# TensorE's order within a head pair: left to the scheduler, or written out in the source

## The chip, the cores and the metric

The kernel runs on one core of one Trainium2 chip. The metric is the device time of one execution, in microseconds (us). A core has TensorE (PE in the profile, for matrix products and transposes), VectorE (DVE), ScalarE (ACT), GpSimd (POOL) and SyncE (SP, which issues most loads). Each works through its own list of instructions and waits at an instruction whose inputs, or whose place to write, are not ready. A product goes from SBUF to one of eight PSUM banks of 128 partitions x 512 fp32; VectorE and ScalarE take it from there.

## What is computed

One decoder layer on 1024 tokens of width 1024, in fp32:

```python
h = rms_norm(x, norm_mix)
xa, ga, q, f, v, g, m_a, m_b = split(h @ w_in)            # 8 x 1024 columns
y_a = rg_lru(conv(xa)) * gelu(ga)                         # gated linear recurrence
f_gate = lb + (1 - lb) * sigmoid(f);  k = (1 - lb) * sigmoid(-f)
o = hgrn2(silu(q), k, log(f_gate), v)                     # 8 heads, state decays by f_gate
y_b = rms_norm_per_head(o) * silu(g)
x = x + (sigmoid(m_a) * y_a + sigmoid(m_b) * y_b) @ w_out
x = x + relu(rms_norm(x) @ w_up)**2 @ w_down
return rms_norm(x, norm_final)
```

In `hgrn2` a query at time t meets a key at an earlier time s through a decay, the product of all gates from s+1 to t, for each of 128 channels.

## The kernel before

The mixer is done in two halves of 512 tokens (`c`), each with four head pairs (`p`), so the main loop (lines 652 to 671) makes eight passes, called pairs here. In each, eight projections of 256 columns are made: `v` and `xa` first, then `q`, `f`, `g`, `mb`, `ga`, `ma`. Every large product is fp32 made of three products of rounded parts (`mm3`, lines 113 to 117, called a triple here): high by high, low by high, high by low. One projection (`project`, line 270) is 48 products of 128x512 into two banks, 24 for each of its two weight tiles. Weight tiles are loaded by SP and split into two parts by ScalarE (a cast, L76) and VectorE (a subtraction, L77); there is room for three split tiles, so a tile is split when the one three places before it in the list `ORDER` (line 29) is used up. These splits have raised priority (400, line 90).

`conv` and `rg_lru` (lines 296 and 326) make the gated recurrence. `rg_lru` has for each of its two heads six products into a bank `pr` and six into a bank `pi`, then ScalarE and VectorE steps on the tiles `rw`, `ri` and `rr`, of which there is one each, so that the second head has to wait for the first. Its instructions have raised priority (300).

`f_of` makes the gate and the key. `hgrn` (line 385) works out the decayed scores at growing block sizes: products for single tokens (`pt1`, L460), for blocks of 2 (`pt2`, L461) and of 8 (`pt8`, L479), 32 small products each; then of 32 (L513, 16 products) and 64 (L525, 8). A product of unrounded fp32 counts as two instructions in the trace. VectorE makes the operands in a chain of multiplications (L388), from one size to the next, and puts the scores together in `dd` with masks (L410, L418). Then, for each head, keys are transposed (`pk`, L551) and copied by ScalarE (`kT`, L553), multiplied with the values to state products (`pkv`, L557), which VectorE adds up to states (`sn`, L571 and L573), and the outputs are made from scores and states (`po`, L564 and L567). ScalarE and VectorE normalise the output (`on`), and it is transposed back (`poT`, L612).

`gates` (line 587) makes the four projections `g`, `mb`, `ga`, `ma` and their nonlinear functions, and joins everything into the mixer's output.

PSUM has four banks under the tag `pj` (projections and `rg_lru`), two under `sc` (scores) and two under `hg` (transposes, states, outputs). A bank is handed on when the last reader of its old contents is through.

What sets the order: the tile framework orders every engine's list when the program is built. An instruction counts as ready by a model of the chip, and among those ready the one earliest in the source (or of raised priority) is taken. So the products of `hgrn` go between the products of `gates` where the model says that their inputs are ready. Only the score blocks are held somewhat: `together` (line 381) puts each block behind one named VectorE instruction, without a wait of its own, so that a block is issued in one piece.

After the eight pairs come the output projection's second half and a feed-forward network in which large products follow each other (from about 915 us on); it is not touched.

## Time and profile before

| | |
|---|---|
| median of 3 runs | 1618.57 us (1615.73 to 1618.93) |
| the profiled execution | 1616.99 us, of it 1615.2 us span from the first to the last instruction |
| PE busy | 1569.3 us in 9240 instructions |
| DVE, ACT, POOL busy | 1214.4, 770.4, 68.0 us |
| one pair | 107.1 us (`q` begins at 148.52 and at 255.63 us) |

A row of the timeline has the start, the duration, engine, line, operation, the tile written and the tiles read, the shape and the number of instructions; in brackets how long the engine was idle before it and what it is thought to have waited for. PE's durations are modelled and overlap: the time that a product takes of the engine is the distance to the next start. A row of the waits has the engine and line that waited, what for, the sum, how many waits, and the longest. A row of the windows has a stretch of the span, its length, then for each engine the busy time and the number of instructions, the granted clock, the share of the DMA engines and GB/s.

### The profile page before, as it was taken

Reading aid. Unit: us, or ns where it says so; the run is one execution under the profiler, and the core shown is the slowest. Engines: PE = TensorE matmul, PEld = TensorE weight load, DVE = VectorE, ACT = ScalarE, POOL = GpSimd, SP = SyncE. Lnnn points to the kernel's source line nnn. Section 1 sums busy time; section 2 is a strip of 40 time slices with the busy share of each in tenths; the row PEclk is TensorE's granted clock in tenths of the full one; section 3 lists DMA queues with packets and bytes.
Section 4 is the critical chain, followed back from the end, with each engine's and each line's share of the span. In section 5 each row is a group of like instructions: output and inputs, shape, how many; then the busy total and the mean of one; then the engine's idle time right before and its main releaser. Section 6 shows DMA issues by size and latency. Waiting matters only on the chain.

```text
span 1615.2 us, 23207 instructions
## 1 busy us (share of the span) xinstructions
PE 1569.3 (97%) x9240; PEld 1306.0 (81%) x9240; DVE 1214.4 (75%) x1751; ACT 770.4 (48%) x1202; POOL 68.0 (4%) x99
## 2 busy tenths in 40 slices
PE   7999999999999999999999997999999999999998
PEld 6878788788788888788788875888888878888886
DVE  5975966848763865947758688888888888788876
ACT  4643545436432544546435476677667732222113
POOL 0010010100100010100100100000000000000000
PEclk9999999999999999999999999999999999999999
DMA  6222223222244222222122362666666575666652
GB/s 238 92 66 92 92 66 103 81 79 91 80 162 138 92 66 92 92 73 97 66 92 92 106 233 78 257 244 242 244 257 242 225 283 214 256 258 249 258 211 105
DMA packets 57996, 246.51 MB, mean 153 GB/s; under 512 B 6688, under 2 KB 6816, under 8 KB 47136
## 3 DMA queue, kind: packets, MB, share of 16 engines
q1 hardware_dynamic: 56304, 239.27, 40.7%
q10 hardware_dynamic: 1584, 5.77, 1.0%
q8 instruction: 72, 1.18, 0.3%
q14 instruction: 36, 0.29, 0.1%
HBM read 185.24 MB, written 59.77 MB: 152 GB/s over the span
## 4 chain that ended last, share of the span: by engine, by line
PE 76%; DVE 20%; DMA 1%; issue 1%; ACT 1%; POOL 0%; DVEq 0%; POOLq 0%; SPq 0%; ACTq 0%
PE dX L115 3%; PE uX L115 3%; PE dX L116 3%; PE dX L117 3%; PE uX L117 3%; PE uX L116 3%; DVE wL L77 3%; PE pv L116 2%; PE pv L117 2%; PE pv L115 2%; PE pj_ma L117 2%; PE pj_ma L115 2%; PE pj_ma L116 2%; PE pj_f L117 2%; PE pj_f L115 2%; PE pj_f L116 2%
## 5 line engine op out<-in xcount | busy, mean ns | idle before, releaser
L77 DVE TENSOR_TENSOR wL<-raw,wH 128x1024 fp32r<-128x1024 f32 x160 | 195.8, 1224 | 136.8 <-ACT wH L76 134.7
L76 ACT CAST wH<-raw 128x1024 fp32r<-128x1024 f32 x160 | 167.8, 1049 | 136.4 <-PE po L116 31.7
L989 DVE TENSOR_TENSOR acc<-acc,dX 128x512 f32<-128x512 f32 x128 | 84.9, 683 | 29.4 <-PE dX L117 29.1
L76 ACT CAST wA<-q 128x512 fp32r<-128x512 f32 x32 | 19.8, 622 | 132.9 <-PE dX L117 101.4
L989 DVE TENSOR_TENSOR acc<-acc,dY 128x512 f32<-128x512 f32 x64 | 43.4, 685 | 15.6 <-PE dY L117 14.6
L345 DVE RECIPROCAL rr<-rr 128x512 f32<-128x512 f32 x16 | 53.5, 3346 | 0.0
L849 ACT ACTIVATE b<-b 128x512 f32<-128x512 f32 x48 | 30.2, 630 | 37.3 <-DVE b L848 37.3
L115 PE MATMUL pv<-wH,hT0H 128*128 128x256 f32 x128 | 37.8, 295 | 0.0
L116 PE MATMUL pv<-wL,hT0H 128*128 128x256 f32 x128 | 37.5, 293 | 0.0
L117 PE MATMUL pv<-wH,hT0L 128*128 128x256 f32 x128 | 37.4, 292 | 0.0
L577 ACT ACTIVATE on<-po 128x128 f32<-128x128 f32 x64 | 17.0, 278 | 41.9 <-PE po L567 41.9
L115 PE MATMUL pv<-wH,hT1H 128*128 128x256 f32 x128 | 36.5, 285 | 0.0
L116 PE MATMUL pv<-wL,hT1H 128*128 128x256 f32 x128 | 36.2, 283 | 0.0
L117 PE MATMUL pv<-wH,hT1L 128*128 128x256 f32 x128 | 36.2, 283 | 0.0
L311 DVE SCALAR_TENSOR_TENSOR xc<-xp,pvt,xc 128x512 f32<-128x512 f32 x48 | 33.1, 745 | 0.0
L596 ACT ACTIVATE smb<-pj_mb 128x512 f32<-128x512 f32 x16 | 9.5, 595 | 46.9 <-PE pj_mb L117 46.9
L850 ACT ACTIVATE b<-b 128x512 f32<-128x512 f32 x48 | 30.0, 630 | 1.1
L491 POOL TENSOR_SCALAR scT<-dd 32x256 f32<-32x256 f32 x32 | 27.6, 863 | 68.3 <-DVE dd L418 66.8
L77 DVE TENSOR_TENSOR wA<-q,wA 128x512 fp32r<-128x512 f32 x32 | 22.0, 687 | 10.4 <-ACT wA L76 9.9
L293 ACT COPY v<-pv 128x256 f32<-128x256 f32 x32 | 11.8, 370 | 30.0 <-PE pv L117 30.0
L116 PE MATMUL pj_ga<-hT0L,wH 128*128 128x512 f32 x64 | 26.1, 408 | 0.0
L117 PE MATMUL pj_ga<-hT0H,wL 128*128 128x512 f32 x64 | 26.1, 408 | 0.0
(1859 smaller groups left out, 5252.2 us busy)
## 6 DMA issues: line engine op xcount, KB each, us to landing
raw<-wts_in SPq DMA_DIRECT2D x160, 512.0 KB, 3.4
q<-mlp_in SPq DMA_DIRECT2D x64, 512.0 KB, 4.0
x<-x_in SPq DMA_DIRECT2D x8, 512.0 KB, 5.6
acc<-x ACTq DMA_DIRECT2D x8, 512.0 KB, 5.5
y_out<-acc SPq DMA_DIRECT2D x16, 256.0 KB, 2.0
xs<-x_in SPq DMA_DIRECT2D x8, 256.0 KB, 3.3
x<-xs SPq DMA_DIRECT2D x8, 256.0 KB, 2.2
x2s<-x_in SPq DMA_DIRECT2D x4, 512.0 KB, 5.1
```

Of the source, the lines that this page charges most:

```text
L76: keep(A.copy(h, src))
L77: keep(V.tensor_tensor(out=lo, in0=src, in1=h.bitcast(F32), op=ALU.subtract))
L115: PE.matmul(o, ah, bh, start=first, stop=False, **how)
L116: PE.matmul(o, ah, bl, start=False, stop=False, **how)
L117: PE.matmul(o, al, bh, start=False, stop=last, **how)
L311: V.scalar_tensor_tensor(xc[:, s, :], xp[:, j : j + T], pvt[:, PV_CW + 8 * j + u : PV_CW + 8 * j + u + 1], xc[:, s, :], op0=ALU.mult, op1= ...
L345: V.reciprocal(rec, rec)
L491: G.tensor_scalar(scT[32 * b : 32 * b + 32, :, 32 * b : 32 * b + 32], dd[32 * b : 32 * b + 32, :, :], 1.0, 0.0, op0=ALU.mult, op1=ALU.add,)
L577: A.activation(on[:, 4 * s + n, :], po[:, n * P : (n + 1) * P], AF.Square, accum_out=ssq[:, 4 * s + n : 4 * s + n + 1])
L849: A.activation(b[:, at, :], b[:, at, :], AF.Relu, scale=-1.0 if at == 2 else 1.0)
L850: A.activation(b[:, at, :], b[:, at, :], AF.Square)
L989: V.tensor_tensor(out=dst, in0=dst, in1=banks[bk, pr], op=op)
```

## The change

TensorE's instructions of a pair, from `q` on to `poT`, are each tied behind the TensorE instruction that stands before it in the source (`pin`, by `keep_in_program_order`); `v` and `xa` are not. `together` goes. The source order is now written out: `project` becomes a generator that stops after every six products (a step; a projection has eight), `gates` becomes one too, and `hgrn` calls `go(n)` to let `gates` go on by n steps. With `GO` this is: `q`; four steps of `f`; `rg_lru`; four steps of `f`; all of `g` and `mb` (16 steps); `pt1`, `pt2`, `pt8`; 5 steps of `ga`; the blocks of 32 and 64; 1 step; the transposes of both heads; 1 step; both state products; 2 steps (the last of `ga`, the first of `ma`); the outputs of both heads; the rest of `ma`; `poT`. What `gates` does with a finished projection on ScalarE and VectorE now stands in the source where the next step is called for.

`f`'s two weight tiles stand on both sides of `rg_lru`'s in `ORDER`. Some tiles change: `pt8` goes to an `hg` bank; `qb` no longer shares a tile with `q1`; the keys of the second size get a tile `kc` of their own, a quarter of which ScalarE copies, where they were made in place in `kb`; the second head's `kT` uses `rr`, and the states use `rw` and `ri`. The last state is copied by GpSimd into `scar`, where VectorE wrote it there. The masks `own_block` and `level_blocks(0)` stand behind the three score blocks.

```diff
-ORDER = ("v", "xa", "q", "f", "rg", "g", "mb", "ga", "ma")
+ORDER = ("v", "xa", "q", "f0", "rg", "f1", "g", "mb", "ga", "ma")
...
+GO = (16, 5, 1, 1, 2)
...
+    pinned = [False]
+
+    def pin(ins):
+        if pinned[0]:
+            tc.keep_in_program_order(ins)
+
     def mm3(o, ah, al, bh, bl, first, last, goes_on=False):
         how = {"skip_group_check": True} if goes_on else {}
-        PE.matmul(o, ah, bh, start=first, stop=False, **how)
-        PE.matmul(o, ah, bl, start=False, stop=False, **how)
-        PE.matmul(o, al, bh, start=False, stop=last, **how)
+        pin(PE.matmul(o, ah, bh, start=first, stop=False, **how))
+        pin(PE.matmul(o, ah, bl, start=False, stop=False, **how))
+        pin(PE.matmul(o, al, bh, start=False, stop=last, **how))
...
-    def project(c, name):
+    def project_steps(c, name):
...
                     mm3(pp[s], wh[:, cols], wl[:, cols], hh, hl, half == 0 and k == 0, half == 1 and k == 3)
+                yield
         return pp
+
+    def run(steps, n=None):
+        while n is None or n > 0:
+            try:
+                next(steps)
+            except StopIteration as end:
+                return end.value
+            if n is not None:
+                n -= 1
+
+    def project(c, name):
+        return run(project_steps(c, name))
...
-        q1 = mt("q1", f"q1{c}{p}", (P, 1792))[:, 0:1536].rearrange("p (a b) -> p a b", b=3)
+        q1 = mt("q1", f"q1{c}{p}", (P, 1536)).rearrange("p (a b) -> p a b", b=3)
...
-    def together(ins, behind):
-        no_sync = mybir.DependencyInfo(mybir.DependencyClass.NoSync, mybir.DependencyReason.DATA)
-        tc.add_manual_dep(ins.ins, behind.ins.name, no_sync, reason="together")
-
-    def hgrn(c, p, q1, f, kk, v):
+    def hgrn(c, p, q1, f, kk, v, go):
...
-        def blocks(k_, rhs, name, behind, tag="sc"):
...
-                    together(
+                    pin(
                         PE.matmul(
                             pt[32 * b : 32 * b + 32, n, :], k_[:, 32 * k : 32 * k + 32], rhs(k), start=True, stop=True
-                        ),
-                        behind,
+                        )
...
-        qb = mt("q1", f"qb{nm}", (P, 1792)).rearrange("p (a b) -> p a b", b=56)
+        qb = mt("qb", f"qb{nm}", (P, 1792)).rearrange("p (a b) -> p a b", b=56)
...
-        behind = level_q(qa, t4, g0, c0)
-        pt1 = blocks(kk, lambda k: q1[:, 16 * k : 16 * k + 16, :], "1", behind)
-        pt2 = blocks(kb, lambda k: qa[:, k * g0 // 32 : (k + 1) * g0 // 32, 1:7, :], str(c0), behind)
-        own_block(pt1)
-        level_blocks(0, c0, pt2)
+        level_q(qa, t4, g0, c0)
         before, after = sums(t4, g0)
-        k4 = kb.rearrange("p (a b c) -> p a b c", b=4, c=c0)
-        mul(k4[:, :, 0:3, :], k4[:, :, 0:3, :], after.unsqueeze(3).to_broadcast([P, g0, 3, c0]))
+        kc = mt("kc", f"kc{nm}", (P, 2 * T))
+        k4 = lambda k, cw: k.rearrange("p (a b c) -> p a b c", b=4, c=cw)
+        A.copy(k4(kc, c0)[:, :, 3, :], k4(kb, c0)[:, :, 3, :])
+        mul(k4(kc, c0)[:, :, 0:3, :], k4(kb, c0)[:, :, 0:3, :], after.unsqueeze(3).to_broadcast([P, g0, 3, c0]))
...
-        behind = level_q(q4, t4, g1, c1)
-        pt8 = blocks(kb, lambda k: q4[:, k * g1 // 32 : (k + 1) * g1 // 32, 1:7, :], str(c1), behind)
+        level_q(q4, t4, g1, c1)
+        go(GO[0])
+        pt1 = blocks(kk, lambda k: q1[:, 16 * k : 16 * k + 16, :], "1")
+        pt2 = blocks(kb, lambda k: qa[:, k * g0 // 32 : (k + 1) * g0 // 32, 1:7, :], str(c0))
+        pt8 = blocks(kc, lambda k: q4[:, k * g1 // 32 : (k + 1) * g1 // 32, 1:7, :], str(c1), "hg")
+        before, after = sums(t4, g1)
+        own_block(pt1)
+        level_blocks(0, c0, pt2)
         level_blocks(1, c1, pt8)
-        before, after = sums(t4, g1)
-        k4 = kb.rearrange("p (a b c) -> p a b c", b=4, c=c1)
-        mul(k4[:, :, 0:3, :], k4[:, :, 0:3, :], after.unsqueeze(3).to_broadcast([P, g1, 3, c1]))
-        kc = kb
+        mul(k4(kc, c1)[:, :, 0:3, :], k4(kc, c1)[:, :, 0:3, :], after.unsqueeze(3).to_broadcast([P, g1, 3, c1]))
...
-        behind = mul(pairs(qf)[:, :, 1, :], q8[:, :, 1, :], t8[:, :, 0:1].to_broadcast([P, 16, 32]))
+        mul(pairs(qf)[:, :, 1, :], q8[:, :, 1, :], t8[:, :, 0:1].to_broadcast([P, 16, 32]))
+        go(GO[1])
...
-                together(
+                pin(
...
                         stop=True,
-                    ),
-                    behind,
+                    )
...
-            together(
+            pin(
...
-                ),
-                behind,
+                )
...
-        pos = []
-        for s in range(2):
-            u = 2 * p + s
-            pk = bank("hg", f"pk{c}{u}")
+        both = [(s, 2 * p + s) for s in range(2)]
+        vn = lambda s, n: v[:, n, s * P : (s + 1) * P]
+        go(GO[2])
+        pk = [bank("hg", f"pk{c}{u}") for _, u in both]
+        for s, _ in both:
             for n in range(nkv):
-                PE.transpose(pk[:, n * P : (n + 1) * P], kk[:, s * T + n * P : s * T + (n + 1) * P], ident)
-            kT = mt("kT", f"kT{c}{u}", (P, 4, P))
-            A.copy(kT[:, :nkv, :], pk[:, : nkv * P].rearrange("p (n k) -> p n k", n=nkv))
-            pkv = bank("hg", f"pkv{c}{u}")
-            vn = lambda n: v[:, n, s * P : (s + 1) * P]
+                pin(PE.transpose(pk[s][:, n * P : (n + 1) * P], kk[:, s * T + n * P : s * T + (n + 1) * P], ident))
+        kT = []
+        for s, u in both:
+            kT.append(mt(("kT", "rr")[s], f"kT{c}{u}", (P, 4, P)))
+            A.copy(kT[s][:, :nkv, :], pk[s][:, : nkv * P].rearrange("p (n k) -> p n k", n=nkv))
+        go(GO[3])
+        pkv = [bank("hg", f"pkv{c}{u}") for _, u in both]
+        for s, _ in both:
             for n in range(nkv):
-                PE.matmul(pkv[:, n * P : (n + 1) * P], kT[:, n, :], vn(n), start=True, stop=True)
-            sn = mt("sn", f"sn{c}{u}", (P, 3, P))
-            state = lambda n: scar[:, u, :] if n in (0, 4) else sn[:, n - 1, :]
-            po = bank("hg", f"po{c}{u}")
+                pin(PE.matmul(pkv[s][:, n * P : (n + 1) * P], kT[s][:, n, :], vn(s, n), start=True, stop=True))
+        states = []
+        for s, u in both:
+            sn = mt(("rw", "ri")[s], f"sn{c}{u}", (P, 4, P))
+            states.append([scar[:, u, :]] + [sn[:, n, :] for n in range(4)])
+            for n in range(nkv):
+                kv = pkv[s][:, n * P : (n + 1) * P]
+                if c == 0 and n == 0:
+                    V.tensor_copy(states[s][1], kv)
+                else:
+                    V.scalar_tensor_tensor(
+                        states[s][n + 1],
+                        states[s][n],
+                        t128[:, 4 * s + n : 4 * s + n + 1],
+                        kv,
+                        op0=ALU.mult,
+                        op1=ALU.add,
+                    )
+        go(GO[4])
+        po = [bank("hg", f"po{c}{u}") for _, u in both]
+        for s, u in both:
             for n in range(4):
                 only = c == 0 and n == 0
-                on_ps = po[:, n * P : (n + 1) * P]
-                PE.matmul(on_ps, scT[:, 4 * s + n, :], vn(n), start=True, stop=only)
+                on_ps = po[s][:, n * P : (n + 1) * P]
+                pin(PE.matmul(on_ps, scT[:, 4 * s + n, :], vn(s, n), start=True, stop=only))
                 if not only:
                     at = s * T + n * P
-                    PE.matmul(on_ps, qf[:, at : at + P], state(n), start=False, stop=True)
-                if n < nkv:
-                    kv = pkv[:, n * P : (n + 1) * P]
-                    if only:
-                        V.tensor_copy(state(1), kv)
-                    else:
-                        V.scalar_tensor_tensor(
-                            state(n + 1), state(n), t128[:, 4 * s + n : 4 * s + n + 1], kv, op0=ALU.mult, op1=ALU.add
-                        )
+                    pin(PE.matmul(on_ps, qf[:, at : at + P], states[s][n], start=False, stop=True))
+            if nkv == 4:
+                G.tensor_copy(scar[:, u, :], states[s][4])
...
-    def gates(c, p, h, on, dst):
-        pg = project(c, f"g{c}{p}")
...
-        pb = project(c, f"mb{c}{p}")
+        pb = yield from project_steps(c, f"mb{c}{p}")
...
-        pa = project(c, f"ga{c}{p}")
+        pa = yield from project_steps(c, f"ga{c}{p}")
...
-        pm = project(c, f"ma{c}{p}")
+        pm = yield from project_steps(c, f"ma{c}{p}")
...
-                PE.transpose(pt[:, n * P : (n + 1) * P], on[:, 4 * s + n, :], ident)
+                pin(PE.transpose(pt[:, n * P : (n + 1) * P], got["on"][:, 4 * s + n, :], ident))
...
-        V.scalar_tensor_tensor(g1, g1, 0.5, h, op0=ALU.mult, op1=ALU.mult)
+        V.scalar_tensor_tensor(g1, g1, 0.5, got["h"], op0=ALU.mult, op1=ALU.mult)
...
+            pinned[0] = True
             q1 = q_of(c, p, project(c, f"q{c}{p}"))
-            f, kk = f_of(c, p, project(c, f"f{c}{p}"))
+            steps = project_steps(c, f"f{c}{p}")
+            run(steps, 4)
+            got = {}
             with tc.high_priority(300):
-                h = rg_lru(c, p, *xc3)
-            on = hgrn(c, p, q1, f, kk, v)
-            gates(c, p, h, on, ys)
+                got["h"] = rg_lru(c, p, *xc3)
+            f, kk = f_of(c, p, run(steps))
+            rest = gates(c, p, got, ys)
+            got["on"] = hgrn(c, p, q1, f, kk, v, lambda n: run(rest, n))
+            run(rest)
+            pinned[0] = False
...
+            elif name[:1] == "f":
+                tiles.append(win[GROUPS["f"] * 4 + p][int(name[1:])][None])
```

More of the change, by code (lines that the diff above doesn't have):

```diff
@@ L389, in hgrn, with blocks @@
         dd = mt("dd", f"dd{nm}", (P, 8, 32))
-        def blocks(k_, rhs, name, behind, tag="sc"):
+        def blocks(k_, rhs, name, tag="sc"):
             pt = bank(tag, f"sc{name}_{nm}")[:, : 8 * 48].rearrange("p (n t) -> p n t", n=8)
@@ L576, in hgrn @@
             for n in range(4):
                 A.activation(
[L578 removed]
+                    on[:, 4 * s + n, :],
+                    po[s][:, n * P : (n + 1) * P],
+                    AF.Square,
+                    accum_out=ssq[:, 4 * s + n : 4 * s + n + 1],
                 )
[L580 removed]
+            A.copy(on[:, 4 * s : 4 * s + 4, :], po[s].rearrange("p (n d) -> p n d", n=4))
@@ L585, in hgrn, with gates @@
         return on
-    def gates(c, p, h, on, dst):
-        pg = project(c, f"g{c}{p}")
+    def gates(c, p, got, dst):
+        pg = yield from project_steps(c, f"g{c}{p}")
         g2 = mt("g2", f"g2{c}{p}", (P, 2, T))
```

4 lines of the change are left out of this document (1 added, 3 removed).

## The prediction

> **What bounds the kernel now.** I read the page's busy times first, then TensorE's waits, then one pair's timeline. The first fence has the page's row of busy times and the row of the chain that ended last; the second has TensorE's waits in the pairs.
>
> ```profile
> PE 1569.3 (97%) x9240; PEld 1306.0 (81%) x9240; DVE 1214.4 (75%) x1751; ACT 770.4 (48%) x1202; POOL 68.0 (4%) x99
> ...
> PE 76%; DVE 20%; DMA 1%; issue 1%; ACT 1%; POOL 0%; DVEq 0%; POOLq 0%; SPq 0%; ACTq 0%
> ```
>
> ```profile
> PE sc L398 <- DVE seg L388: 6.9, 8, 0.9
> ...
> PE sc L398 <- ACT qb L469: 4.5, 8, 0.6
> ...
> PE sc L525 <- DVE qf L388: 1.6, 7, 0.2
> ...
> PE sc L525 <- ACT scT L531: 0.9, 1, 0.9
> ...
> PE pr L115 <- DVE q L365: 0.8, 1, 0.8
> ...
> PE sc L513 <- DVE qb L388: 0.3, 1, 0.3
> ```
>
> TensorE sets the time: it is 97% busy. The change adds no product and takes none away, so it can only win TensorE's waits and the price of going to and fro between large and small products. The waits in the pairs are 6.9 + 4.5 + 1.6 + 0.9 + 0.8 + 0.3 = 15.0 us in eight pairs, 1% of the span. I take the second pair (`q` to the end of `ga`) as the measure, cut in two where the third score block is done and `mb` is over; the windows view cuts there, and its third stretch is that of VectorE's chain to `pt8`.
>
> ```profile
> 159.40:202.21 42.81, 41.38 (x362) 33.54 (x361) 39.42 (x63) 22.76 (x30) 2.21 (x4) 1.00 0.27 87
> 202.21:221.46 19.25, 19.01 (x150) 16.10 (x149) 10.86 (x21) 9.85 (x30) 4.75 (x5) 1.00 0.18 57
> 164.50:199.99 35.49, 34.20 (x271) 27.83 (x269) 35.32 (x56) 19.24 (x24) 2.21 (x4) 1.00 0.25 82
> ```
>
> In the third stretch VectorE is busy for 35.32 of 35.49 us. So in the first part of the pair TensorE and VectorE run side by side, both full; that is what the change meets. TensorE's rows of this pair:
>
> ```profile
> 159.40 0.39 PE L115 MATMUL pj_f<-hT0H,wH 128*128 128x512 f32 x1
> 159.63 0.39 PE L116 MATMUL pj_f<-hT0L,wH 128*128 128x512 f32 x1
> ...
> 160.53 0.50 PE L115 MATMUL pr<-xcH,wH 128*128 128x512 f32 x1
> ...
> 162.81 0.39 PE L115 MATMUL pi<-xcH,wH 128*128 128x512 f32 x1
> ...
> 200.13 0.89 PE L398 MATMUL sc<-qb,kb 128*32 128x48 f32 x64 [0.86 <-DVE seg L388]
> 200.95 0.50 PE L116 MATMUL pj_mb<-hT0L,wH 128*128 128x512 f32 x1
> ...
> 205.71 0.70 PE L513 MATMUL sc<-qb,kb 128*32 128x32 f32 x32
> 206.65 1.12 PE L525 MATMUL sc<-qf,kk 128*64 128x64 f32 x16 [0.24 <-DVE qf L388]
> 207.69 0.50 PE L115 MATMUL pj_ga<-hT0H,wH 128*128 128x512 f32 x1
> ...
> 208.72 0.60 PE L551 MATMUL pk<-ident,kk 128*128 128x128 f32 x4
> 209.08 0.48 PE L116 MATMUL pj_ga<-hT0L,wH 128*128 128x512 f32 x1
> 209.40 0.40 PE L117 MATMUL pj_ga<-hT0H,wL 128*128 128x512 f32 x1
> ...
> 210.10 1.06 PE L557 MATMUL pkv<-v,kT 128*128 128x128 f32 x8
> 210.99 0.61 PE L564 MATMUL po<-v,scT 128*128 128x128 f32 x4
> ```
>
> A large product takes 159.63 - 159.40 = 0.227 us, a step of six 1.36, a projection 10.88. A score block takes 200.95 - 200.13 = 0.82, the block of 32 0.70 (its duration), that of 64 207.69 - 206.65 = 1.04, four transposes 0.36, eight instructions of `pkv` 0.89, so 0.11 each. The first large product after small ones takes 209.40 - 209.08 = 0.32: a return costs about 0.1.
>
> **First part: `q`'s end to the third score block.** *TensorE alone.* 48 products of `f`, 24 of `rg_lru`, 96 of `g` and `mb` are 168 x 0.227 = 38.1 us; three blocks are 2.46, one return 0.1: 40.65, against 42.81 now. The difference of 2.16 is the most this part can win: 0.86 and the 0.56 of the second block (4.5 over 8) are waits, the rest returns and the blocks' other pauses.
>
> *What the pin at `f` costs.* Now `rg_lru` begins 1.13 us after `q` (160.53) and its first bank of six products is full at 162.81, 3.41 after. Pinned, it comes behind four steps: full at 5.44 + 1.36 = 6.80, so 3.39 later. The recurrence begins there, and both engines behind it are late by as much:
>
> ```profile
> 163.01 0.69 ACT L337 ACTIVATE rw<-pr,pvt 128x512 f32<-128x512 f32 x1 [2.05 <-PE pr L117]
> ...
> 174.35 0.70 ACT L340 ACTIVATE ri<-pi,pvt 128x512 f32<-128x512 f32 x1
> ```
>
> ```profile
> 164.50 0.43 DVE L342 TENSOR_SCALAR rw<-rw 128x512 f32<-128x512 f32 x1 [2.17 <-ACT rw L338]
> ...
> 169.16 1.16 DVE L77 TENSOR_TENSOR wL<-raw,wH 128x1024 fp32r<-128x1024 f32 x1
> ...
> 171.90 1.22 DVE L77 TENSOR_TENSOR wL<-raw,wH 128x1024 fp32r<-128x1024 f32 x1
> 173.03 1.28 DVE L352 TENSOR_TENSOR_SCAN h<-rr,hcar,ri 128x512 f32<-128x512 f32 x1
> ...
> 194.25 0.41 DVE L388 TENSOR_TENSOR dd<-sc,mf 128x256 f32<-128x256 f32 x1
> ...
> 198.01 0.28 DVE L418 COPY_PREDICATED dd<-mu,sc 128x64 f32<-128x64 uint8 x1
> ```
>
> *A new wait at `g`.* Of the four `pj` banks `f` keeps two across `rg_lru`, so both heads of `rg_lru` share the other two, and `g` needs exactly those. They come free when ScalarE has read the second head's `pr` and `pi`; that needs `rw` and `ri` back from the first head, the last by the scan. From the first ScalarE row (163.01) to the last (174.35) are 11.34 us, with two weight splits of about 1.1 in it. With `f`'s first tile free before the recurrence starts, one of them falls into VectorE's earlier idle time: 10.2. The last read is then at 163.01 + 3.39 + 10.2 = 176.6, over at 177.4 with its 0.7 and a handover of 0.1. TensorE reaches `g` at 159.40 + 72 x 0.227 = 175.7, can do three products in the bank of `pr`, and then waits from 176.4 to 177.4: 1.0. Behind it on TensorE stand all of `g`, `mb` and the blocks. If the second split stays inside, it is 2.1; if VectorE and ScalarE catch up, nothing. A gain is excluded, since `g` has no wait now. I take 1.3, near the row-by-row value, and keep 0 and 2.1.
>
> *The wait at `pt8`.* `pt1` and `pt2` have their operands long before; only the last block waits for VectorE. VectorE starts 3.39 later, does the same 35.49 us, less one split (1.1) and less the five mask instructions from 194.25 to 198.01, which now come after the blocks (durations 0.41 to 0.28 by their first and last row, less overlap: about 1.2). Its last operand is ready at 199.99 + 3.39 - 2.3 = 201.1. TensorE with the wait at `g` stands before `pt8` at 159.40 + 38.1 + 1.3 + 1.65 = 200.45. So `pt8` runs from about 201.2 to 202.0, the first part takes 42.6, and wins 0.2. If the two products of `g` (L592), which stand in the source behind the chain now, are really put there, VectorE is ready sooner and TensorE's own 200.45 + 0.82 decides: 41.9, a gain of 0.9. I take 0.5.
>
> **Second part: `ga` and what is between it.** By the rows: 48 products 10.88, blocks of 32 and 64 1.74, eight transposes 0.72, sixteen instructions of `pkv` 1.78, 28 of `po` 3.1, so 18.2; now it takes 19.25, of which 0.24 is a wait and 0.8 are eight returns. Pinned there are four returns: 18.6. What hides the work between is now fixed. *Blocks of 32 and 64* stand five steps behind `pt8` (6.8 us); VectorE needs now 6.5 us from 199.99 to the last multiplication, and gets 1.2 of masks on top: 7.7, of which 0.9 lies beside `pt8`, against 6.8 + 0.7 of cover until the block of 64: no wait, with half a us in hand. *`pkv`* stands one step (1.36) and the other head's transposes (0.36) behind the first transposes; ScalarE's copy takes 0.59, and a weight cast of 1.05 just before it makes that 1.64: between nothing and a few tenths, up to 1.0 with both copies late. *Outputs* stand two steps behind `pkv`, 2.7 + 0.9 for eight additions to the states of 0.35 each: hidden. Rows for these, and for the last output and `on` below:
>
> ```profile
> 209.36 0.59 ACT L553 COPY kT<-pk 128x512 f32<-128x512 f32 x1 [0.98 <-PE pk L551]
> 210.30 1.04 ACT L76 CAST wH<-raw 128x1024 fp32r<-128x1024 f32 x1 [0.35 <-PE pj_ga L116]
> ```
>
> ```profile
> 218.24 0.39 PE L567 MATMUL po<-sn,qf 128*128 128x128 f32 x2
> ```
>
> ```profile
> 205.62 0.88 DVE L388 TENSOR_TENSOR qf<-qb,seg 128x512 f32<-128x512 f32 x1
> ...
> 213.07 0.34 DVE L573 SCALAR_TENSOR_TENSOR sn<-sn,seg,pkv 128x128 f32<-128x128 f32 x1
> ...
> 221.85 1.22 DVE L388 TENSOR_TENSOR on<-on,hrs 128x1024 f32<-128x1024 f32 x1 [1.84 <-POOL hrs L583]
> ```
>
> I take 0.35 of waits: 18.95, a gain of 0.3, with 0 and 1.4 as ends.
>
> **What costs nothing.** `ma` and `poT`: the pinned outputs end seven steps (9.5 us) before `poT`, and the way from the last output to the normalised `on` is 4.7 us now (218.4 to 223.1, from the rows above). ScalarE's quarter copy into `kc` and GpSimd's two copies into `scar` fall on engines that are 48% and 4% busy; nobody waits for `scar` within the half. `rr`, `rw` and `ri` as homes of `kT` and the states are free some 40 us after `rg_lru` and given back before the next pair's. Loads on SP are the same number of tiles in another order. `v` and `xa`, not pinned, cannot slip forward: their weight tiles come behind `ma`'s.
>
> **The sum.** 0.5 + 0.3 = 0.8 a pair, eight pairs: 6.4 us. The profiled execution took 1616.99, so 1610.6. The median of the runs is 1.6 above that execution; against it the forecast is 1612.2, and I give 1612. About 0.2%, 3.2 us, is what a measurement of this kernel can tell from no change.
>
> **The rivals.** *Nearly all is won.* If VectorE catches up in its idle time before the recurrence and the wait at `g` vanishes, a pair wins 2.16 + 0.65 = 2.8: 22 us, about 1595. VectorE's 35.32 of 35.49 busy speaks against it. *The waits only move.* The wait at `g` is 2.1 and `pkv` waits 1.0: 1615 to 1619. The same comes out if the pins change little, for instance because the order stays near the present one. *Slower: VectorE becomes the bound at `pt8`.* If the two products of `g` stay ahead of the chain, as now, and the next weight split (raised priority, 1.1) falls before its last two multiplications, `pt8` begins at 202.3 and the first part takes 43.7, 0.9 more than now; the second part's margin of half a us turns into a wait of 1 at the block of 64, 19.5, 0.3 more than now. 1.2 a pair are 10 us: 1622 to 1630. It decides from where `pt8` starts later than 42.3 us after `q`'s end, since then the 0.3 of the second part no longer make up for it. For it: VectorE has no slack, and a pinned TensorE cannot fill the time with other products. Against: five masks have left the chain.
>
> *Slower by the clock.* The granted clock is 1.00 in all three stretches above, with waits of 0.24 to 0.86 us in the first two. A longer wait in the midst of `g` could lower it behind the wait: one step per pair whose products take twice their 0.227 us costs 8 x 1.36 = 11 us, and the change ends near 1622. It decides from waits longer than the 0.86 us that the trace shows without harm. The Trainium skill, "TensorE: Matmul & The Clock Gate", section "A second HAM failure mode: psum-queue depth-cycling", says that frequent short idles between groups of products can make TensorE's clock swing between half and full. By that rule the present waits would already cost clock; the trace does not agree, with its 1.00, so I give it little.
>
> **Chances.** The forecast (1606 to 1615) 0.45; nearly all won 0.12; waits only move 0.20; slower by VectorE 0.20; slower by the clock 0.03. So faster 0.57, same 0.20, slower 0.23. The range leaves out the best part of the first rival and the worst of the slower ones: 1600 to 1626. The forecast's own range is 1606 to 1618.
>
> **What would show it.** `pr` begins 5.4 us after `q`. TensorE waits at `g` for ScalarE's `ri` by 0.5 to 2.1 us in every pair; the waits at the score blocks of now (11.4 us) fall under 4. The stretch from `q`'s end to the third block takes 41.9 to 42.6, the next 18.6 to 19.5, a pair 106 to 106.8. I am wrong at `g` if no wait stands there; in the chain's sum if `pt8` waits more than 1 us; in the cover if `pkv` or the block of 64 waits more than 1 us.

## The result, and the profile after

| | before | after |
|---|---|---|
| median of 22 runs each | 1617.63 us (1615.73 to 1619.84) | 1616.31 us (1613.90 to 1621.96) |
| ratio | | 0.9996 (95% interval 0.9989 to 1.0002) |
| the profiled execution, its span | 1616.99, 1615.2 us | 1615.42, 1613.6 us |
| PE busy | 1569.3 us | 1565.5 us |

The change cannot be told from no change. The forecast was a win of 6.4 us; the spans of the two profiled executions differ by 1.6.

The page of the changed kernel, in the order of the page: the busy times, the DMA queue that carries instructions (packets, MB, share), and the shares of the chain that ended last.

```profile
PE 1565.5 (97%) x9240; PEld 1305.6 (81%) x9240; DVE 1206.9 (75%) x1751; ACT 773.1 (48%) x1210; POOL 64.8 (4%) x107
...
q8 instruction: 72, 1.18, 0.3%
...
PE 90%; DVE 5%; ACT 2%; DMA 2%; issue 1%; POOL 0%; DVEq 0%; POOLq 0%; SPq 0%; ACTq 0%
```

VectorE's share of the chain falls from 20% to 5%: TensorE hangs on VectorE far less. TensorE's waits in the pairs of the changed kernel:

```profile
PE pj_g L122 <- ACT ri L360: 9.5, 8, 1.2
...
PE sc L414 <- issue: 5.5, 4, 1.7
```

The 15.0 us of waits for score operands and `q` are gone. In their place stand two: 9.5 us at `g` in all eight pairs, which the forecast has, and 5.5 us at the score blocks in four pairs, which it has not. That one has "issue" as its releaser: TensorE waited for no engine and no transfer of data.

The second pair on TensorE, VectorE and ScalarE (one fence for each view: first TensorE's timeline, then VectorE's first step of the recurrence and its last operand of `pt8`, then ScalarE's last read of `rg_lru`'s banks):

```profile
157.70 0.39 PE L122 MATMUL pj_f<-hT0H,wH 128*128 128x512 f32 x1
...
163.14 0.39 PE L122 MATMUL pr<-xcH,wH 128*128 128x512 f32 x1
...
176.30 0.50 PE L122 MATMUL pj_g<-hT0H,wH 128*128 128x512 f32 x1 [1.16 <-ACT ri L360]
...
197.62 0.89 PE L414 MATMUL sc<-q,kk 128*32 128x48 f32 x64
198.32 0.88 PE L414 MATMUL sc<-qa,kb 128*32 128x48 f32 x64
199.24 0.89 PE L414 MATMUL sc<-qb,kc 128*32 128x48 f32 x64
```

```profile
166.24 0.43 DVE L362 TENSOR_SCALAR rw<-rw 128x512 f32<-128x512 f32 x1 [0.77 <-ACT rw L358]
...
198.40 0.70 DVE L404 TENSOR_TENSOR qb<-qb,seg 128x512 f32<-128x512 f32 x1
```

```profile
175.57 0.67 ACT L360 ACTIVATE ri<-pi,pvt 128x512 f32<-128x512 f32 x1
```

VectorE's last operand is ready at 198.40 + 0.70 = 199.10, and the third block begins at 199.24: it still follows VectorE closely, though no wait is listed there. The windows of that pair, cut where the third block ends; the first goes from `q`'s end to there, the second to `poT`:

```profile
157.70:200.06 42.36, 41.16 (x362) 33.42 (x360) 37.35 (x56) 24.48 (x33) 2.48 (x4) 1.00 0.26 88
200.06:229.75 29.69, 29.69 (x204) 25.35 (x198) 20.00 (x35) 13.52 (x34) 5.00 (x7) 1.00 0.19 63
```

Before, the first was 42.81 and the second, up to `poT`, 30.13:

```profile
202.21:232.34 30.13, 29.89 (x198) 25.05 (x196) 18.63 (x28) 14.85 (x37) 5.11 (x5) 1.00 0.18 57
```

So the pair wins 0.45 + 0.44 = 0.89. Pairs of the first half last 106.22 us (`q` at 146.82 and 253.04) against 107.1, and up to the output projection between the halves 5.3 us are won (it begins at 443.09, before at 448.37). In the second half the pairs take 107.4, 107.9 and 109.5 (`q` at 513.36, 620.80, 728.65 and 838.18), and of the 5.3 us 1.6 are left at the end. **So the loss is in the second half.** The timeline of its score blocks, the place where TensorE starts again in each pair, and one pair whole:

```profile
567.45 0.62 PE L414 MATMUL sc<-qb,kc 128*32 128x48 f32 x37 [1.19 <-issue]
...
675.43 0.50 PE L414 MATMUL sc<-qb,kc 128*32 128x48 f32 x26 [1.61 <-issue]
...
779.42 0.89 PE L414 MATMUL sc<-q,kk 128*32 128x48 f32 x64
780.12 0.88 PE L414 MATMUL sc<-qa,kb 128*32 128x48 f32 x64
781.04 0.76 PE L414 MATMUL sc<-qb,kc 128*32 128x48 f32 x50
783.46 0.37 PE L414 MATMUL sc<-qb,kc 128*32 128x48 f32 x14 [1.67 <-issue]
...
892.53 0.28 PE L414 MATMUL sc<-qb,kc 128*32 128x48 f32 x3 [1.09 <-issue]
```

TensorE stops in the midst of the third block, with 37, 26, 14 and 3 of its 64 instructions still to come, that is after 155, 166, 178 and 189 of the 192. The place moves by 11 or 12 from pair to pair: nothing in the data does that. Behind the longest stop the clock is down for a while; the windows view, with the granted clock in the third column from the end:

```profile
779.40:783.76 4.36, 2.65 (x193) 2.33 (x192) 4.33 (x12) 1.48 (x3) 0.03 (x1) 1.00 0.09 30
783.76:787.20 3.44, 3.44 (x15) 2.74 (x10) 3.44 (x9) 1.08 (x2) 0.00 (x0) 0.59 0.40 146
787.20:791.00 3.80, 3.80 (x17) 3.05 (x16) 1.50 (x6) 0.23 (x2) 1.59 (x4) 0.92 0.00 0
```

Missing are 0.41 x 3.44 + 0.08 x 3.80 = 1.7 us of full clock; the five steps of `ga` there take 8.64 us against 7.02 in a pair without it. Together with the 5.5 us of stops that is 7.2 us. With 0.89 in each of the last four pairs the change would have won 5.3 + 3.6 = 8.9 us, and it won 1.6: this accounts for what is missing.

### The profile page after: what moved, and what is told of

The parts are those of the page before. It is cut to its first block, busy times and chain, and to the rows that moved or that the text cites. A ratio compares the mean times of both kernels' runs of the same rounds, so it can differ in the third digit from the quotient of the medians.

```text
span 1613.6 us, 23213 instructions
## 1 busy us (share of the span) xinstructions
PE 1565.5 (97%) x9240; PEld 1305.6 (81%) x9240; DVE 1206.9 (75%) x1751; ACT 773.1 (48%) x1210; POOL 64.8 (4%) x107
## 3 DMA queue, kind: packets, MB, share of 16 engines
q8 instruction: 72, 1.18, 0.3%
## 4 chain that ended last, share of the span: by engine, by line
PE 90%; DVE 5%; ACT 2%; DMA 2%; issue 1%; POOL 0%; DVEq 0%; POOLq 0%; SPq 0%; ACTq 0%
PE dX L122 3%; PE uX L122 3%; PE dX L123 3%; PE dX L124 3%; PE uX L124 3%; PE uX L123 3%; PE pj_ga L122 2%; PE pj_ga L124 2%; PE pj_ga L123 2%; PE pj_g L122 2%; PE pj_ma L124 2%; PE pj_ma L122 2%; PE pj_xa L122 2%; PE pj_f L123 2%; PE pj_xa L123 2%; PE pj_ma L123 2%
## 5 line engine op out<-in xcount | busy, mean ns | idle before, releaser
L122 PE MATMUL pj_g<-hT1H,wH 128*128 128x512 f32 x64 | 25.8, 403 | 4.8 <-ACT ri L360 4.8
L122 PE MATMUL pj_g<-hT0H,wH 128*128 128x512 f32 x64 | 25.8, 404 | 4.7 <-ACT ri L360 4.7
L122 PE MATMUL pj_ga<-hT1H,wH 128*128 128x512 f32 x64 | 27.3, 426 | 0.0
L122 PE MATMUL pj_ga<-hT0H,wH 128*128 128x512 f32 x64 | 26.6, 416 | 0.0
L124 PE MATMUL pj_ga<-hT1H,wL 128*128 128x512 f32 x64 | 25.7, 401 | 0.0
```

Of the source, the lines that this page charges most:

```text
L122: pin(PE.matmul(o, ah, bh, start=first, stop=False, **how))
L124: pin(PE.matmul(o, al, bh, start=False, stop=last, **how))
```

## The theories

**A: instruction loading.** The page has 72 packets and 1.18 MB on the instruction queue, 16 KB each. TensorE runs 9240 products and 9240 weight loads, 18,480 instructions; over 72 that is 257. So its instructions come in blocks of 256. A pair is about 1513 of them, 5 x 256 + 233, so a block's end moves 23 instructions, 11.5 products, further into the stretch from pair to pair: this is the step from 155 to 189. The joint score blocks are 384 instructions in 2.44 us. The stops at 155 to 189 products are at about 310, 333, 356 and 379 instructions; by A these are block ends, and the one before lies 256 earlier, at 54 to 123, inside the same stretch, with only 256 x 2.44/384 = 1.6 us between them. In the third of these pairs TensorE starts again at 783.46, 3.4 us after the first block end (some 50 products after 779.42); in the four pairs this time is 2.8 to 3.4 us. The trace's records of single packets fit: in each of the four pairs one packet on the instruction queue begins inside the stretch (at 565.07, 673.20, 781.01 and 890.36), and TensorE starts again 2.2 to 2.5 us after it begins. In the first half, counted back along the trace's list of instructions, only one end falls into each stretch (at 172 to 229). Before the change the small products came in pieces, and among large ones 256 instructions last 128 x 0.227 = 29 us.

**B, its rival: something of the second half's data or memory** (other loads at that time, other weight tiles) holds TensorE, whatever stands where in its list.

**C: the pin at `f`.** That `rg_lru` is held behind four steps of `f` makes VectorE late, costs the wait at `g`, and takes the larger part of what the new order wins. Its rival, D: VectorE is full in the first part of the pair and takes the gain anyway, wherever `rg_lru` stands.

## The experiments

All ratios are against the kernel before on the same chip.

**1 and 2. Shift the instructions.** Tiny products, whose results nobody reads, move every later block end:

```diff
+    def fill_in(n):
+        pt = bank("hg", "fill_in")
+        for _ in range(n):
+            tc.keep_in_program_order(
+                PE.matmul(pt[0:32, 0:1], ident[:, 0:32], ident[:, 0:1], start=True, stop=True)
+            )
...
         ys = a2_set(a2y, f"y{c}")
+        if c == 1:
+            fill_in(36)
```

> 36 tiny products are put into TensorE's list between the two halves, 144 instructions; their result is used by nobody. Theory (instruction loading): TensorE's list comes in blocks of 256 instructions; in the second half two block ends, 256 apart, fall into the 384 instructions of the joint score block (after 54, 77, 100 and 123 instructions, by the trace's counts), and the second block is not there in time. Shifted by 144, only one falls in: the four waits put down to issue (5.5 us) go, the pairs of the second half take 106.2 instead of 107 to 109.5 us, no clock dip follows them; less about 1 us for the products, 1610 to 1612. Rival (the wait belongs to the second half, its data, banks or transfers): the four waits stay, 1616 to 1618.

In the second run `fill_in(35)` stands instead behind `pinned[0] = True` of the very first pair.

> 35 tiny products, 140 instructions, before the first pair's queries. Theory (instruction loading): the block ends move in all pairs. In the first half the first of them now falls after 32, 51, 70 and 89 instructions of the joint score block, where it was after 172 to 229, so that a second one falls in; in the second half the first falls before the block. So the waits change halves: pairs 0 to 3 each get 1 to 2 us put down to issue, pairs 4 to 7 none; the time stays near 1616 to 1618. Rival (the wait belongs to the second half): pairs 4 to 7 keep their four waits, pairs 0 to 3 get none.

The first: 1611.38 us, ratio 0.9965 (0.9952 to 0.9978), and no stop in any pair. The same stretch as shown above, on its timeline:

```profile
780.03 0.89 PE L414 MATMUL sc<-q,kk 128*32 128x48 f32 x64
780.73 0.88 PE L414 MATMUL sc<-qa,kb 128*32 128x48 f32 x64
781.65 0.89 PE L414 MATMUL sc<-qb,kc 128*32 128x48 f32 x64
```

The second: 1617.68 us, ratio 1.0004 (0.9996 to 1.0013). The stops go to the first half, where there had been none, and the second half has none:

```profile
98.25 0.72 PE L414 MATMUL sc<-qb,kc 128*32 128x48 f32 x48 [0.73 <-issue]
206.22 0.63 PE L414 MATMUL sc<-qb,kc 128*32 128x48 f32 x39 [1.44 <-issue]
313.90 0.54 PE L414 MATMUL sc<-qb,kc 128*32 128x48 f32 x29 [1.09 <-issue]
422.02 0.45 PE L414 MATMUL sc<-qb,kc 128*32 128x48 f32 x20 [1.52 <-issue]
```

With 48, 39, 29 and 20 left they stand after 144, 153, 163 and 172 products, where A puts the shifted block ends (288, 307, 326 and 345 instructions). Position in the list decides, not the half: A holds, B falls. It also shows why the change's own time is partly chance: 140 instructions more or fewer anywhere ahead decide which pairs pay.

**3. One step between the second and the third block** (`GO[0]` 15, `go(1)` ahead of `pt8`):

> The first two score blocks one step earlier (after 15 steps), then one step of six large products, then the third block where it was. Theory (instruction loading): between two block ends there are now at least 1.4 us more; the waits inside the score blocks fall from 5.5 us to under 1, the clock dip goes; one return more per pair costs 0.8 in all: 1609 to 1612, about 0.35% faster than the kernel before. Rival (VectorE's chain is what the third block really waits for): 1.2 to 1.7 us per pair of the second half stay, at the third block: 1616 to 1618.

1613.77 us, ratio 0.9980 (0.9972 to 0.9989). TensorE's waits in the pairs:

```profile
PE pj_g L122 <- ACT ri L360: 9.5, 8, 1.2
...
PE sc L414 <- issue: 2.6, 4, 1.1
```

The stops fall from 5.5 to 2.6, not under 1, and the time lies above the 1609 to 1612 expected: a miss in size. 1.36 us of large products between the two block ends would have covered more if the loading time were fixed; here it took 3.5 to 4.3 us from the first block end to the restart. From the start of the packet to the restart it is 2.2 to 2.4 us, as in the changed kernel, so the packet starts later here. In the DMA records it starts right behind a 512 KB weight load in two of these pairs, so it may queue behind data; that was not tried by itself.

**4. `rg_lru` after two steps of `f`** (`run(steps, 2)`):

> The recurrence's products after two steps of f, not four; the rest as in the changed kernel. Theory (the wait at g comes from the late start of the recurrence): its bank reads end 2.7 us sooner, the eight waits at g (9.5 us) go; pr waits 0 to 0.4 us for the queries' banks instead (0 to 3 us in all); VectorE's chain begins sooner too, so no new wait at the third block: 1607 to 1611. Rival (ScalarE's own order sets the wait at g): it stays near 1.2 us a pair, 1616.

1607.18 us, ratio 0.9940 (0.9929 to 0.9952). The wait at `g` is gone, and another has come; TensorE's waits at the score blocks:

```profile
PE sc L414 <- DVE qb L404: 9.4, 8, 1.2
...
PE sc L414 <- issue: 0.4, 2, 0.2
```

The time is as expected, the statement that nothing new would wait is not. TensorE arrives earlier by the 1.16 us and VectorE by only 0.6, so the third block waits 1.17 us a pair for its operand. That pause lets the instructions come, and the stops nearly vanish beneath it.

**5. No pins.** Everything stays but the line that turns the pins on:

```diff
-            pinned[0] = True
```

> The change without its pins: the source order, tiles, buffers and the early loads stay, but no instruction of TensorE is held to its place, so the order within a pair is chosen from priorities as before. If the pins are what wins the 0.89 us of a first-half pair, as the theory has it, the pairs take about 107 us again, the waits at the score blocks are back with some 8 to 15 us in sum, the wait at g (1.2 a pair) is gone or smaller, since rg_lru slips forward again, and no wait of the kind 'issue' above 1 us in sum stands in the second half, because the score blocks come apart: 1614 to 1622. The rival, that the moved masks, the new tiles and the copies bring the 0.89 and the pins cost or do nothing, gives pairs of 106.2 or less and a time of 1605 to 1612.

1604.44 us, ratio 0.9915 (0.9901 to 0.9928): 11.9 us under the changed kernel by the medians. The main statement fell, and the time is even a little under the rival's range. Without pins the blocks do stand together, and `pk`, `pkv` and `po` stand where the source has them: TensorE's list differs from the changed kernel's only among the products of `f` and `rg_lru`. VectorE's and ScalarE's lists change with it, by some weight splits and steps of the recurrence, so what follows is the price of that pin with all that hangs on it. The raised priority of `rg_lru` pulls it forward to the first step of `f`. The second pair on TensorE's timeline:

```profile
157.64 0.39 PE L122 MATMUL pj_f<-hT0H,wH 128*128 128x512 f32 x1
157.87 0.49 PE L122 MATMUL pr<-xcH,wH 128*128 128x512 f32 x1
...
195.30 0.89 PE L414 MATMUL sc<-q,kk 128*32 128x48 f32 x64
196.00 0.87 PE L414 MATMUL sc<-qa,kb 128*32 128x48 f32 x64
196.68 0.88 PE L414 MATMUL sc<-qb,kc 128*32 128x48 f32 x64
```

VectorE's first step of the recurrence and its last operand of `pt8` there:

```profile
161.07 0.43 DVE L362 TENSOR_SCALAR rw<-rw 128x512 f32<-128x512 f32 x1 [1.18 <-ACT rw L358]
...
195.24 0.70 DVE L404 TENSOR_TENSOR qb<-qb,seg 128x512 f32<-128x512 f32 x1
```

And the two windows, cut as above:

```profile
156.96:197.49 40.53, 40.53 (x361) 33.31 (x360) 38.10 (x57) 24.64 (x33) 2.87 (x4) 1.00 0.28 92
197.49:227.22 29.73, 29.73 (x203) 25.35 (x197) 19.76 (x34) 13.51 (x34) 5.22 (x7) 1.00 0.19 61
```

TensorE is busy for 40.53 of 40.53 us: no wait is left. The recurrence starts 161.07 - 156.96 = 4.1 us after `q`'s end; in the changed kernel it was 8.5 (166.24 - 157.70). VectorE is through 0.7 us before `pt8` needs it. The pair takes 104.44 us (`q` at 146.08 and 250.52), 1.78 less than with the pins and 2.67 less than before. C holds, D falls: VectorE is busy 38.10 of the 40.53 us and keeps nobody waiting. The stops remain, in the same four places, and three of them are longer (1.81, 1.61, 2.02, 2.02):

```profile
PE sc L414 <- issue: 7.5, 4, 2.0
```

Eight times 1.78 is 14.2 us. The 2.0 us more of stops, one more stretch at half the clock behind a stop (1.7) and a wait of 0.9 in the first pair take 4.6 of it; that leaves 9.6, against 8.7 between the two profiled spans (1613.6 and 1604.9) and 11.9 between the medians.

**6. No pins, with the shift** (the `fill_in(36)` of the first experiment):

> The version without pins, with 36 tiny products (144 instructions) between the two halves, whose results nobody reads. Without pins the score blocks stand together as in the changed kernel and wait for instructions in the same four pairs of the second half (1.6 to 2.0 us each, 7.5 in sum, with two or three stretches at half the clock behind them). By the theory of the instruction loading all of that goes: no wait of the kind 'issue' in the score blocks, second-half pairs of 104.4 to 104.8 us as in the first half, 1604.4 - 7.5 - 1 to 2 + 0.6: 1594 to 1598. If the early rg_lru itself makes the pauses, they stay and the time is 1604 to 1606.

1598.12 us, ratio 0.9874 (0.9859 to 0.9890), the fastest of all kernels here by its median, and just above the 1594 to 1598 expected. No stop is left; a pair of the second half on the timeline, by the first product of `q` in two pairs:

```profile
719.88 0.39 PE L122 MATMUL pj_q<-hT1H,wH 128*128 128x512 f32 x1
...
824.15 0.39 PE L122 MATMUL pj_q<-hT1H,wH 128*128 128x512 f32 x1
```

That is 104.27, against 106.1 to 108.1 without the shift. The tiny products cost more than the 0.6 I gave them, 4 us: 2.37 themselves, and 1.57 because the products of `v` behind them run at a lower clock (windows; the same 96 products take 11.52 us without them):

```profile
485.04:487.41 2.37, 2.37 (x74) 2.35 (x73) 1.23 (x1) 0.93 (x1) 0.00 (x0) 0.99 0.50 182
487.41:500.50 13.09, 13.09 (x99) 13.09 (x97) 1.66 (x3) 2.17 (x4) 0.00 (x0) 0.87 0.37 121
```

**7. No pins, one step between the second and the third block** (`go(1)` ahead of `pt8`, `GO[1]` 4):

> The version without pins, with one step of a projection between the second and the third score block. As in the version with rg_lru after two steps the step of 1.36 us gives the loading time: its waits fall from 7.5 us to 1 to 3 in sum, at the price of one more return (0.1 a pair, 0.8): 1597 to 1601. If VectorE, not the loading, sets the second half, the time stays at 1603 to 1606.

1601.36 us, ratio 0.9901 (0.9888 to 0.9915); the stops fall to 1.2 us in sum. The time is just above the upper edge of what was expected.

**8 and 9. What the new order wins without pins.** The first two blocks go back to where they were, a third into `mb`; in 8 with their masks, in 9 with the masks left behind the third block:

```diff
         level_q(qa, t4, g0, c0)
+        go(10)
+        pt1 = blocks(kk, lambda k: q1[:, 16 * k : 16 * k + 16, :], "1")
+        pt2 = blocks(kb, lambda k: qa[:, k * g0 // 32 : (k + 1) * g0 // 32, 1:7, :], str(c0))
+        own_block(pt1)
+        level_blocks(0, c0, pt2)
         before, after = sums(t4, g0)
...
-        go(GO[0])
+        go(6)
```

> The version without pins, with the first two score blocks again a third and a half into the projection of mb, and their five mask instructions on VectorE again ahead of the chain to the third block, as before the change; the third block alone at its place, everything else as changed. If taking the masks out of VectorE's chain is what wins the first part of a pair, the third block waits again for VectorE: its operand, which comes 0.7 us ahead of it without pins, comes 1.2 us later, so 0.5 us of wait and 0.2 for two returns: first-half pairs of 105.0 to 105.3 against 104.44. The pauses for instruction loading go, since the blocks stand apart, so the time is 1597 to 1602 all the same. If the masks do not matter, the pairs are 104.5 to 104.7 and the time is 1595 to 1597.

> The version without pins with the first two score blocks at their earlier place, a third and a half into mb, as in the version before it, but with their five mask instructions left behind the third block as in the changed kernel. That version lost 1.6 us a pair against the one with the blocks together (106.05 against 104.44), with a wait of 0.8 at the second block and none at the third. If the place of the blocks is what costs, a first-half pair is 105.8 to 106.1 again and the time 1605 to 1609. If the masks in VectorE's chain are what costs, the wait at the second block stays at most 0.3 and the pair is 104.6 to 105.1: 1597 to 1601.

1608.38 us, ratio 0.9940 (0.9928 to 0.9953), with the masks; 1608.43 us, 0.9946 (0.9932 to 0.9959), without. A first-half pair takes 106.04 and 106.02 us on the mean of two (147.75 to 359.83 and 147.68 to 359.72), and in both TensorE waits in front of the second block, here in the one without masks:

```profile
PE sc L414 <- DVE qa L404: 6.5, 8, 0.8
```

My expectation for 8 was wrong: I had looked for a wait at the third block. With the masks ahead or behind the pair takes the same time, so they cost nothing in this order. That holds without pins; in the changed kernel, where the third block follows VectorE's operand within 0.14 us, it was not tried. It is the place of the first two blocks that is worth 106.04 - 104.44 = 1.6 us a pair, 0.8 of it a wait for VectorE, the rest not taken apart (two more returns are about 0.2). The other 1.07 us of the 2.67, from 107.11 to 106.04, come from what 8 and 9 leave as changed (the rest of the order, the tiles and copies) and were not taken apart either.

**10 to 12. Pinned, but better placed.** `rg_lru` after two steps throughout. In the first, one step between the second and third block (`go(1)`, `GO[1]` 4); in the second, all blocks one step later (`GO` = 17, 4, 1, 1, 2); in the third, this and `fill_in(36)`:

> The version with rg_lru after two steps, and one step of a projection between the second and the third score block; the block of 32 stays where it was, counted in steps. TensorE has then 1.36 us of large products before the third block, where it waits 1.17 us for VectorE in the version with two steps. If that wait is VectorE's and fixed in time, it falls to 0 to 0.2 a pair and 8 x 1.0 to 1.2 us = 8 to 9.4 us are won; the instruction loading, hidden behind that wait until now (0.4 us in sum), shows again, but with a projection's step between as in the version with the third block apart: 1.5 to 3 us in sum. So 1600 to 1603. If the wait moves on instead (to the block of 32 or 64, since VectorE is the bound), the time stays at 1606 to 1608.

> The version with rg_lru after two steps, and all three score blocks one step later, still as one. The wait for VectorE at the third block (1.17 a pair, 9.4 us in sum) falls to 0 to 0.2. The three blocks are then one stretch of 384 short instructions again without a pause. By the theory of the instruction loading its second block end falls 149, 160, 172 and 184 products into the stretch in the four pairs of the second half (six products earlier than in the changed kernel, as 12 instructions more stand ahead), and there TensorE stands for 1.1 to 1.7 us each, 5 to 6 us in sum, perhaps with one stretch at half the clock: 1602 to 1606. If the pauses of the changed kernel came from something else that the earlier rg_lru removed, none stands there: 1597 to 1600.

> The same as the version before it, with 36 tiny products (144 instructions) between the two halves, whose results nobody reads. By the theory of the instruction loading no pause of the kind 'issue' is left in the score blocks, since no stretch of any pair holds two block ends close to one another; the time is 5 to 7 us under that of the version without the tiny products: 1597 to 1600. If the pauses depend on something other than the position in the instruction stream, they stay and the time is the same, or 0.5 us more for the tiny products.

1599.09 us, ratio 0.9886 (0.9873 to 0.9900); 1602.99, 0.9910 (0.9897 to 0.9924); 1601.19, 0.9899 (0.9885 to 0.9912). The first is a little under the 1600 to 1603 expected, with stops of 1.1 us in sum, and its second pair takes 104.81 us, as that of experiment 7 does without pins: it is the place of `rg_lru` that costs, not that the order is held. The wait for VectorE at the third block is gone in all three. In the second the stops are back, six products earlier than in the changed kernel, as A says; two of the four:

```profile
667.63 0.55 PE L414 MATMUL sc<-qb,kc 128*32 128x48 f32 x32 [1.37 <-issue]
...
773.42 0.45 PE L414 MATMUL sc<-qb,kc 128*32 128x48 f32 x20 [1.39 <-issue]
```

With 32 and 20 left, these are 160 and 172 products in. In the third none is left, but its time was expected at 1597 to 1600: between the halves the tiny products cost 2.6 us (`q` to `q` 156.70 against 154.12), and the block of 64 waits for VectorE by 3.3 us in sum, 1.9 more than in the second. The first is the best kernel that does no needless work, and its runs lie within 1 us (1598.59 to 1599.53).

## Why the prediction was right or wrong

**Right, by its rows.** The forecast was 1612 with a range of 1606 to 1618, and 1616.31 lies within it. `pr` begins 163.14 - 157.70 = 5.44 us after `q`; the wait at `g` is for ScalarE's `ri` and takes 1.16, between the row-by-row 1.0 and the 1.3 taken; VectorE's last operand is ready 41.4 us after `q`'s end (forecast 201.1 - 159.40 = 41.7); the first part takes 42.36 (42.3); the second, up to `poT`, wins 0.44 (0.3), with no wait at `pkv` or the block of 64. The pair wins 0.89 where the sum says 0.8, as long as no stop falls into it. That the time of the whole lies in the range is partly luck: what keeps it near the upper end is not in the prediction, and a shift of the list by 144 instructions brings 1611.38, though its tiny products cost 4.0 us (`q` to `q` between the halves 158.0 against 154.0). The rival "the waits only move" also has the number (1615 to 1619), but not the cause: the wait at `g` is 1.16, not 2.1, and `pkv` does not wait.

**Wrong: the sum leaves out what the joined blocks cost TensorE itself.** The step that failed is the price of the score blocks in "TensorE alone": three blocks at 0.82 each, 2.46 us, taken from blocks that stood apart. The same three in one stretch cost 2.46 plus 1.1 to 1.7 us in those pairs where two block ends of the instruction list fall into it, 5.5 us in four pairs, plus 1.7 of clock behind one stop. The step priced durations and waits for data, and the "What costs nothing" part named other engines and the loads, but not the queue that brings TensorE's own instructions. It stood on the page (72 packets, 1.18 MB), and 384 instructions in 2.46 us follow from "counts as two instructions" and PEld's count.

**The clock rival was a real mechanism with another trigger.** A stretch at half pace happened once in the profiled execution, for 1.7 us, behind a stop of 1.67. The forecast let it begin at a wait in `g`: those of 1.16 us do no harm, all eight. Nor does length alone decide: without pins one stop of 2.02 us was followed by a stretch at half pace and the other was not.

**"Nearly all is won" was dismissed for a poor reason.** "VectorE's 35.32 of 35.49 busy speaks against it", I wrote. Without the pin at `f` the first part takes 40.53 us, even under the 40.65 that the prediction worked out for TensorE alone, with VectorE 94% busy, and the pair wins 2.67, against 2.8 in that rival. A busy chain that starts earlier ends earlier. The prediction priced the pin at `f` rightly as a delay of 3.4 us for VectorE, but it did not ask what the rest of the change would be worth without it: 1.78 us a pair more. Where the win came from was mixed up too: the masks, which I took as 1.2 us off VectorE's chain, bring nothing without pins, and the place of the first two blocks brings 1.6.

So the small result is a sum of large parts: the change without its pins wins 2.67 us a pair (21 us) where no stop falls in, the pin at `f` takes 1.78 back (14 us), and the instruction loading with its clock 7 us more, from the 0.89 that is left.

## What to carry to other kernels

Where small products are gathered into one stretch, count its instructions, weight loads included, and compare their time with the time that a block of instructions needs to arrive (here 2.8 to 3.4 us from one block's end to the restart, up to 4.3 in a variant); a step of large products in between is cheap cover. Before the order of one engine is fixed by hand, ask of every fixed instruction who starts behind it: a chain on another engine that feeds the critical one wants to start as early as it can, and a raised priority that did this unasked is lost under a pin. A change that nets nothing is worth taking apart, since here some 21 us of gain lay beneath some 20 of new costs.

## What the runs showed of the hardware

TensorE's instructions arrive in blocks of 256, and a list of short products can outrun them. The Trainium skill, "Runtime: NRT & Kernel Launch", section "Instruction fetch mechanics", says the same of the block, and that crossing its end is mostly hidden. The first agrees (18,480 over 72 is 257). The second agrees for all but four of the 72 blocks of the changed kernel; at those four TensorE stood for 1.1 to 1.7 us, up to 2.02 without pins, where the block end before lay 1.6 us back.

Short stretches of small products can bring the clock to half for about 3.4 us, after a stop (0.59 over 3.44 us) and also with none: 2.37 us of tiny products were followed by 0.87 over the next 13.09 us. Neither is sure. Of the four kernels with tiny products, experiment 12's shows no such dip behind them. Of the eight stops in the changed kernel and the one without pins, five have none, and the joined score blocks (2.44 us) have none where no stop falls in. What decides stays open.
